# A decoder trunk on one core: the per-layer projection moved to the kernel's start, and the form buffers and filler matmuls dealt out anew

## The chip, the core and the metric

One core of one Trainium2 chip. The time is device microseconds of one execution; several executions are taken, and the median is given. The engines are TensorE (PE, its weight loads PEld), VectorE (DVE), ScalarE (ACT), GpSimd (POOL) and SyncE (SP), each with its own queue of instructions, worked off in order; SP, ACT and POOL also issue transfers between DRAM and on-chip memory.

## What is computed

Two layers over 1024 tokens of width 1024, all in float32:

```python
for i in range(DEPTH):
    h = rms_norm(x, norm_mix_g[i])
    z = h @ w_in[i]
    u_conv, q, k, v, g = jnp.split(z, splits, axis=-1)
    conv_out = conv_module(u_conv, ...)        # gate, 31-tap causal convolution, layer norm, silu
    ret = chunkwise_retention(q, k, v, positions)
    ...                                        # group norm of ret, times silu(g)
    mix = jnp.concatenate([conv_out, ret_out], axis=-1) @ w_out[i]
    x = x + mix
    h = rms_norm(x, norm_ffn_g[i])
    x = x + jnp.square(jax.nn.relu(h @ w_ff1[i])) @ w_ff2[i]
    h = rms_norm(x, norm_ple_g[i])
    x = x + jax.nn.sigmoid(h @ w_ple_gate[i]) * (p[i] @ w_ple_proj[i])
return rms_norm(x, final_norm_g)
```

The last line of a layer is the per-layer input: `p[i]`, 256 wide, goes through the projection `w_ple_proj`, and a gate made from the normed x multiplies it. The projection depends on nothing but inputs.

## The kernel before

The tokens are two halves, A and B, of 512. x stays on chip, feature-major, as `x_0` and `x_1` (8 feature blocks of 128 by 512 tokens each). Every float32 product is made of three matmuls of rounded parts (`mm3`, lines 238 to 240: high by high, high by low, low by high), 128x512 each. A weight tile of 128x1024 is loaded by SP (`stage_weight`, L220, into one of two `stage` buffers), and `split` makes its high part on ACT (`w_hi`, L215) and its low part on DVE (`w_lo`, L216), two buffers each. `gemm` (L242) runs the matmuls of one output block of 512 tokens: 24 for a full depth of 1024, 6 for the projection.

The order of instructions on every engine is fixed when the program is built: a scheduler orders them by priority and dependence, `background(d)` moves a piece d places back or, negative, ahead, and within an engine the order stays as it came out. Tiles come from pools with a number of buffers; a tile that has none free waits until an older one has been read for the last time.

A layer in the order of `run` (L713 on): the norm for mixing; `proj_ab`, v, k, q and g of half A, then of half B, with the convolution on DVE beside them; retention; `w_out` of half A and, later, of half B, with the first 20 (`PRE`) of the 32 `ff1` blocks of half A ahead of the latter. `ff1` writes relu squared to `hid` in DRAM (ACT issues, L537). Then 8 more `ff1` of half A, 4 of half B, the last 4 of half A, and `change(1, 0)` (L776): 4 `ff1` of half B, in whose shade `forms` loads the two halves' `hid` through POOL (L546) and builds seven sums and differences, split in high and low parts (`slots`: q11, t1, t2, q21, t4, t3, q22, L561 to L573). `ff2_chunk` then makes, with seven products in place of eight, one chunk of the second feed-forward matmul, and `pair_weights` prepares the matching sums of its weights (`s_hi`, `s_lo`, L593 to L596). In `ff_forms` (L539) the first four slots are buffers of the pool `h`, which the norms' results use too, and the last three are of the pool `form`.

At the end of a layer comes the per-layer stage: `load_p` (L668), `ple_proj` with 2 weight tiles, both halves, 96 matmuls, its results copied into 16 `pr` tiles (L687), then 8 gate blocks for half A and 8 for half B (`ple`, L693). While the projection runs, the norm of half A (`h3A`, begun in the last feed-forward chunk) is finished on ACT and DVE.

The start has a path of its own. `setup` loads the first half's tokens once more, token-major, into `h` tiles (`x_in`), with the first two weights between them, and then `x_1`; `x_0` follows later (`load_x(0)`). `norm_first` (L312) takes the square sums on ACT, the power on POOL, scales the tokens on DVE, and has PE transpose them (L331) for two quarters of 256 tokens; `proj_ab` of block 0 runs in two parts of 256 columns, so that PE starts on the first quarter while the second is loaded. `gates` holds the instructions behind which the two first weights are split. The other norms (`norm`, L298) square x on ACT (L256), add on DVE (L263), and sum over the partitions on PE; in the form `quick` the row sums go through one short chain of PE (L272), DVE (L275), POOL (L276), ACT and DVE (L277, L278), and a broadcast matmul on PE (L279).

## Time and profile before

| | |
|---|---|
| median of 3 executions | 2421.72 us (2420.17 to 2422.37) |
| the profiled execution | 2422.64 us |
| its span | 2420.9 us |
| mean granted clock of TensorE | 0.997 |
| PE busy | 2380.3 us, 98% |
| DVE busy | 1846.6 us, 76% |
| ACT busy | 1091.3 us, 45% |
| POOL busy | 78.8 us, 3% |

The span runs from the first to the last instruction, and the profiled execution's time is 1.74 us longer. A row of the timeline gives the start, the duration, the engine, the line and the tiles, and in brackets how long the engine had been idle and what ended that. A matmul's duration overlaps the next one's; the distance of two starts is what one costs.

### The profile page before, as it was taken

Reading aid. Unit: us, or ns where it says so; the run is one execution under the profiler, and the core shown is the slowest. Engines: PE = TensorE matmul, PEld = TensorE weight load, DVE = VectorE, ACT = ScalarE, POOL = GpSimd, SP = SyncE. Lnnn points to the kernel's source line nnn. Section 1 sums busy time; section 2 is a strip of 40 time slices with the busy share of each in tenths; the row PEclk is TensorE's granted clock in tenths of the full one; section 3 lists DMA queues with packets and bytes.
Section 4 is the critical chain, followed back from the end, with each engine's and each line's share of the span. In section 5 each row is a group of like instructions: output and inputs, shape, how many; then the busy total and the mean of one; then the engine's idle time right before and its main releaser. Section 6 shows DMA issues by size and latency. Waiting matters only on the chain.

```text
span 2420.9 us, 29197 instructions
## 1 busy us (share of the span) xinstructions
PE 2380.3 (98%) x10916; PEld 1951.7 (81%) x10916; DVE 1846.6 (76%) x3182; ACT 1091.3 (45%) x1766; POOL 78.8 (3%) x120
## 2 busy tenths in 40 slices
PE   8999999999999999999999999999999999999998
PEld 7887888888788787888888888888887888878887
DVE  8999999344567677788999999972626777778888
ACT  5335344534544444445542353463445444444454
POOL 1000000000000000000000000000000000000000
PEclk9999999999999999999999999999999999999999
DMA  5322223434433333332222222244354333333424
GB/s 200 100 70 79 79 77 124 139 109 153 157 122 122 113 122 122 113 120 73 95 96 96 64 89 67 87 132 146 107 165 134 123 120 121 119 115 111 131 78 149
DMA packets 89438, 274.81 MB, mean 114 GB/s; under 512 B 9856, under 2 KB 13952, under 8 KB 89296
## 3 DMA queue, kind: packets, MB, share of 16 engines
q1 hardware_dynamic: 59136, 203.45, 26.7%
q10 hardware_dynamic: 20736, 35.66, 4.4%
q0 software_dynamic: 9424, 33.84, 4.3%
q8 instruction: 85, 1.39, 0.2%
q14 instruction: 57, 0.47, 0.1%
HBM read 235.17 MB, written 37.75 MB: 113 GB/s over the span
## 4 chain that ended last, share of the span: by engine, by line
PE 56%; DVE 17%; issue 15%; DMA 7%; ACT 3%; POOL 1%; POOLq 0%; DVEq 0%; ACTq 0%
PE ps_mm L239 17%; PE ps_mm L238 17%; PE ps_mm L240 17%; DVE conv_acc L367 4%; DVE w_lo L216 4%; DMA stage<-in_wts_dram 3%; DMA h<-hid 3%; DVE h L216 2%; DMA hid<-tmp 1%; ACT w_hi L215 1%; PE ps_ret L238 1%; PE ps_ret L239 1%; PE ps_ret L240 1%; POOL gn_rs L502 1%; DVE ftmp L568 1%
## 5 line engine op out<-in xcount | busy, mean ns | idle before, releaser
L238 PE MATMUL ps_mm<-h,w_hi 128*128 128x512 f32 (+1 forms) x2208 | 854.9, 387 | 0.1
L240 PE MATMUL ps_mm<-h,w_lo 128*128 128x512 f32 (+1 forms) x2208 | 853.4, 387 | 1.4 <-DVE w_lo L216 1.3
L239 PE MATMUL ps_mm<-h,w_hi 128*128 128x512 f32 (+1 forms) x2208 | 853.4, 387 | 0.0
L215 ACT CAST w_hi<-stage 128x1024 fp32r<-128x1024 f32 (+1 forms) x368 | 375.2, 1019 | 647.4 <-PE ps_mm L239 441.9
L216 DVE TENSOR_TENSOR w_lo<-stage,w_hi 128x1024 fp32r<-128x1024 f32 (+1 forms) x368 | 434.3, 1180 | 190.2 <-ACT w_hi L215 189.4
L240 PEld LDWEIGHTS ps_mm<-h,w_lo 128*128 128x128 f32 x2208 | 415.5, 188 | 84.5 <-DVE w_lo L216 3.2
L238 PEld LDWEIGHTS ps_mm<-h,w_hi 128*128 128x128 f32 x2208 | 415.6, 188 | 80.9 <-ACT h L332 0.4
L239 PEld LDWEIGHTS ps_mm<-h,w_hi 128*128 128x128 f32 x2208 | 415.6, 188 | 80.4
L367 DVE SCALAR_TENSOR_TENSOR conv_acc<-u,cw,conv_acc 128x512 f32<-128x512 f32 x480 | 340.6, 747 | 2.5
L238 PE MATMUL ps_mm<-w_hi,h 128*128 128x512 f32 x384 | 150.5, 392 | 0.0
L239 PE MATMUL ps_mm<-w_lo,h 128*128 128x512 f32 x384 | 150.3, 391 | 0.0
L240 PE MATMUL ps_mm<-w_hi,h 128*128 128x512 f32 x384 | 150.2, 391 | 0.0
L256 ACT ACTIVATE ntmp<-x 128x256 f32<-128x256 f32 x208 | 81.6, 414 | 86.4 <-DVE ntmp L263 35.8
L593 DVE TENSOR_TENSOR ftmp<-stage 128x256 f32<-128x256 f32 x56 | 23.8, 425 | 95.8 <-DMA stage<-in_wts_dram 95.7
L215 ACT CAST h<-htmp 128x256 fp32r<-128x256 f32 x176 | 66.8, 407 | 49.2 <-DVE htmp L307 48.6
L215 ACT CAST s_hi<-ftmp 128x1024 fp32r<-128x1024 f32 x56 | 58.9, 1051 | 63.9 <-DVE ftmp L596 47.9
L238 PEld LDWEIGHTS ps_mm<-w_hi,h 128*128 128x128 f32 x384 | 72.1, 188 | 14.5
L239 PEld LDWEIGHTS ps_mm<-w_lo,h 128*128 128x128 f32 x384 | 72.3, 188 | 14.3
L240 PEld LDWEIGHTS ps_mm<-w_hi,h 128*128 128x128 f32 x384 | 72.1, 188 | 14.4
L536 ACT ACTIVATE tmp<-tmp 128x512 f32<-128x512 f32 x128 | 81.1, 634 | 3.4
L216 DVE TENSOR_TENSOR s_lo<-ftmp,s_hi 128x1024 fp32r<-128x1024 f32 x56 | 68.5, 1224 | 18.1 <-ACT s_hi L215 17.9
L263 DVE TENSOR_TENSOR ntmp<-ntmp 128x256 f32<-128x256 f32 x176 | 73.8, 419 | 3.9 <-ACT ntmp L256 1.9
(204 smaller groups left out, 3202.1 us busy)
## 6 DMA issues: line engine op xcount, KB each, us to landing
stage<-in_wts_dram SPq DMA_DIRECT2D x368, 512.0 KB, 3.6
hid<-tmp ACTq DMA_DIRECT2D x128, 256.0 KB, 3.2
h<-hid POOLq DMA_DIRECT2D x36, 512.0 KB, 5.0
raw<-hid POOLq DMA_DIRECT2D x28, 512.0 KB, 4.8
x<-in_xT_dram SPq DMA_DIRECT2D x4, 1024.0 KB, 10.5
h<-in_x_dram SPq DMA_DIRECT2D x4, 512.0 KB, 5.4
tmp<-in_pT_dram SPq DMA_DIRECT2D x8, 256.0 KB, 3.0
out_dram<-x SPq DMA_DIRECT2D x16, 128.0 KB, 1.9
```

Of the source, the lines that this page charges most:

```text
L215: self.nc.scalar.copy(hi, src)
L216: self.nc.vector.tensor_sub(lo, src, hi.bitcast(F32))
L238: mm(ps, lhsT=wh, rhs=xh, start=start, stop=False)
L239: mm(ps, lhsT=wh, rhs=xl, start=False, stop=False)
L240: mm(ps, lhsT=wl, rhs=xh, start=False, stop=stop)
L256: square = lambda k, out: nc.scalar.activation(out, self.x[k][h][:, cs], AF.Square)
L263: nc.vector.tensor_add(sq, acc, sq)
L367: nc.vector.scalar_tensor_tensor(acc, u[:, j:j + HT], w(j), acc, ALU.mult, ALU.add)
L502: nc.gpsimd.tensor_tensor(rs, rs, self.npow[:, 0:HEADS], ALU.pow)
L536: nc.scalar.activation(r, r, AF.Square)
L568: sub(a, r21, b)
L593: nc.vector.tensor_add(blk(s, 0), blk(st, 0), blk(st, 3))
```

## The change

It drops the token-major input, `norm_first`, `gates` and the two-part `proj_ab`. The kernel now begins with p of layer 0 and the whole projection of layer 0, whose results are written to DRAM (`prd`); `x_0` and `x_1` are loaded feature-major and half A's first norm is the common one in the form `quick`. Layer 0's per-layer stage makes half of layer 1's projection (first weight tile) and stores it through a pool `prs` of two buffers, and each per-layer stage reads its stored results back through POOL. Layer 1's stage makes the other half there. Of the slots, q11, t1 and q21 now lie in the pool `form`, and t2, t4, t3, q22 in `h`. 16 `ff1` of half A stand ahead of half B's `w_out` in place of 20, and 8 in place of 4 between half B's first four and `change(1, 0)`.

```diff
-PRE = 20
+PRE, SPARE = 16, 8
...
     def weight(self, L, t):
-        first = bool(self.next_weights)
-        st = self.next_weights.pop(0) if first else self.stage_weight(L, t)
+        st = self.stage_weight(L, t)
...
-    def proj_ab(self, L, h, hs, cb, parts=1):
...
+    def proj_ab(self, L, h, hs, cb):
+        nc = self.nc
+        psb = self.gemm(self.weight(L, T_AB + 2 * cb), hs)
+        psa = self.gemm(self.weight(L, T_AB + 2 * cb + 1), hs)
...
     def ff_forms(self):
-        quads = [self.quad()[0] for _ in range(KEPT)]
-        quads += [self.pools["form"].tile([P, 4, HT], F32R, name="form") for _ in range(FORMS - KEPT)]
+        old = [self.quad()[0] for _ in range(KEPT)]
+        new = [self.pools["form"].tile([P, 4, HT], F32R, name="form") for _ in range(FORMS - KEPT)]
+        quads = [new[0], new[1], old[0], new[2]] + old[1:]
...
+    def ple_proj(self, L, pps, i, pool):
+        w = self.weight(L, T_PROJ + i)
+        pr = []
+        for h in range(NH):
+            for m in range(4):
+                ps = self.gemm(w, pps[h], 2 * m)
+                t = self.tile(pool)
+                self.nc.scalar.copy(t, ps)
+                pr.append(t)
         return pr
+
+    def ple_proj_out(self, L, pps, i, pool):
+        for n, t in enumerate(self.ple_proj(L, pps, i, pool)):
+            self.nc.scalar.dma_start(out=self.prd[L][n // 4][4 * i + n % 4], in_=t)
+
+    def ple_proj_in(self, L, h, m):
+        t = self.tile("pr")
+        self.nc.gpsimd.dma_start(out=t, in_=self.prd[L][h][m])
+        return t
...
-                if L > 0:
+                if L == 0:
+                    pps = [self.load_p(0, 0, "gen")]
+                    self.load_x(0)
+                    pps.append(self.load_p(0, 1, "gen"))
+                    self.load_x(1)
+                    self.load_tables()
+                    for i in range(2):
+                        self.ple_proj_out(0, pps, i, "gen")
+                    h1[0] = self.norm(0, V_MIX, 0, True)
+                else:
                     norm_b()
...
-                for m in range(PRE, NMB - 4):
+                for m in range(PRE, NMB - SPARE):
                     self.ff1(L, m, h2[0], hids[0])
                 self.right_pools(raw=2)
                 for m in range(4):
                     self.ff1(L, m, h2[1], hids[1])
-                for m in range(NMB - 4, NMB):
+                for m in range(NMB - SPARE, NMB):
                     self.ff1(L, m, h2[0], hids[0])
...
-            with self.stage_pools(pp=8, pr=16):
-                pr = self.ple_proj(L, [self.load_p(L, h) for h in range(NH)])
+            with self.stage_pools(pp=8, pr=16, prs=2):
+                pps = [self.load_p(1, h, "pp") for h in range(NH)]
+                if L == 0:
+                    self.ple_proj_out(1, pps, 0, "prs")
+                    pr = [[self.ple_proj_in(0, h, m) for m in range(KB)] for h in range(NH)]
+                else:
+                    pr = [[self.ple_proj_in(1, h, m) for m in range(4)] for h in range(NH)]
+                    more = self.ple_proj(1, pps, 1, "pr")
+                    pr = [pr[h] + more[4 * h:4 * h + 4] for h in range(NH)]
                 h3B = self.norm(1, v0 + V_PLE, SLACK)
```

How the order on the engines moves is shown at three places; the changed kernel's lines have numbers of their own (its L223 to L225 are `mm3`, L257 and L264 the row sums and the broadcast of `quick`, L206 and L207 `split`, L292 `htmp`, L640 the copy of a projection result, L646 its store). A number behind a tile's name tells its instances apart.

PE at the start of the kernel, before: transposes of the first quarter, then `proj_ab` in 256 columns with the second quarter's transposes among its matmuls, then the first of 512 columns (block 1).

```order
L331 MATMUL ps_mm<-ident,h 128x128 x16
L238 MATMUL ps_mm<-h,w_hi 128x256
L239 MATMUL ps_mm<-h,w_hi 128x256
L240 MATMUL ps_mm<-h,w_lo 128x256
...
L331 MATMUL ps_mm<-ident,h 128x128 x6
L238 MATMUL ps_mm<-h,w_hi 128x256 x2
...
L238 MATMUL ps_mm<-h,w_hi 128x512
```

PE at the start, changed (`gen` holds the parts of p, `h` the normed x; `w_hi_204` and `w_hi_290` are the projection's two weights, 512 and 543 those of block 0):

```order
L257 MATMUL ps_aux_378<-ones32_111,ntmp_399 128x1 x2
L264 MATMUL ps_ret_406<-ntmp_405,ones32_111 128x256
L223 MATMUL ps_mm_208<-gen_166,w_hi_204 128x512
L224 MATMUL ps_mm_208<-gen_167,w_hi_204 128x512
L223 MATMUL ps_mm_217<-gen_166,w_hi_204 128x512
L225 MATMUL ps_mm_208<-gen_166,w_lo_205 128x512
...
L224 MATMUL ps_mm_357<-gen_187,w_hi_290 128x512
L225 MATMUL ps_mm_357<-gen_186,w_lo_291 128x512
L257 MATMUL ps_aux_444<-ones32_111,ntmp_465 128x1 x2
L264 MATMUL ps_ret_472<-ntmp_471,ones32_111 128x256
L223 MATMUL ps_mm_516<-h_374,w_hi_512 128x512
L223 MATMUL ps_mm_547<-h_374,w_hi_543 128x512
```

The row sums and the broadcast of the first quarter now stand ahead of the projection, those of the second quarter behind its last matmul, and `proj_ab` of block 0 behind both.

DVE around the change-over to the second feed-forward matmul of layer 0, before. `h_5366` and 5367, 5368 are q11, t1, t2; `form_5370` to 5372 are t4, t3, q22; `w_lo_5378`, 5384, 5433, 5474 belong to the four `ff1` of `change`.

```order
L216 TENSOR_TENSOR w_lo_5378<-stage_5375,w_hi_5377 128x1024
L561 TENSOR_TENSOR ftmp_5393<-raw_5387,h_5366 128x1024
L216 TENSOR_TENSOR w_lo_5384<-stage_5381,w_hi_5383 128x1024
L562 TENSOR_TENSOR ftmp_5394<-raw_5388,ftmp_5393 128x1024
L216 TENSOR_TENSOR h_5366<-h_5366 128x1024
L216 TENSOR_TENSOR h_5367<-ftmp_5393,h_5367 128x1024
L216 TENSOR_TENSOR h_5368<-ftmp_5394,h_5368 128x1024
L216 TENSOR_TENSOR w_lo_5433<-stage_5430,w_hi_5432 128x1024
...
L216 TENSOR_TENSOR form_5370<-ftmp_5438,form_5370 128x1024
L216 TENSOR_TENSOR w_lo_5474<-stage_5471,w_hi_5473 128x1024
...
L216 TENSOR_TENSOR form_5371<-ftmp_5479,form_5371 128x1024
L216 TENSOR_TENSOR form_5372<-raw_5388,form_5372 128x1024
```

Changed: `form_5572` to 5574 are q11, t1, q21, `h_5568` to 5571 are t2, t4, t3, q22; `w_lo_5291` and 5536 belong to the first and the last of the eight `ff1` of half A there, 5580 and 5586 to the first two of `change`.

```order
L207 TENSOR_TENSOR w_lo_5291<-stage_5288,w_hi_5290 128x1024
L515 TENSOR_TENSOR ftmp_5595<-raw_5589,form_5572 128x1024
L207 TENSOR_TENSOR form_5572<-form_5572 128x1024
L207 TENSOR_TENSOR form_5573<-ftmp_5595,form_5573 128x1024
...
L207 TENSOR_TENSOR form_5574<-form_5574 128x1024
...
L207 TENSOR_TENSOR w_lo_5536<-stage_5533,w_hi_5535 128x1024
L207 TENSOR_TENSOR w_lo_5580<-stage_5577,w_hi_5579 128x1024
L207 TENSOR_TENSOR h_5568<-ftmp_5596,h_5568 128x1024
L207 TENSOR_TENSOR h_5569<-ftmp_5640,h_5569 128x1024
...
L207 TENSOR_TENSOR w_lo_5586<-stage_5583,w_hi_5585 128x1024
L207 TENSOR_TENSOR h_5570<-ftmp_5681,h_5570 128x1024
L207 TENSOR_TENSOR h_5571<-raw_5590,h_5571 128x1024
```

The first subtraction moved from behind the first weight of `change` to behind the first of eight weights of half A, and the last form from behind the fourth weight of `change` to behind its second.

ACT in the per-layer stage of layer 0, before (`pr` the copies of projection results, `h` the casts of half A's norm, `w_hi_9294` the first gate's weight):

```order
L687 COPY pr_9022<-ps_mm_9015 128x512
L215 CAST h_8657<-htmp_8779 128x256
L215 CAST h_8658<-htmp_8732 128x256
L687 COPY pr_9031<-ps_mm_9024 128x512
L215 CAST h_8657<-htmp_8783 128x256
...
L687 COPY pr_9049<-ps_mm_9042 128x512
L215 CAST h_8658<-htmp_8799 128x256
L215 CAST h_8658<-htmp_8803 128x256
L215 CAST w_hi_9294<-stage_9292 128x1024
L687 COPY pr_9058<-ps_mm_9051 128x512
L687 COPY pr_9073<-ps_mm_9066 128x512
L215 CAST h_8658<-htmp_8807 128x256
```

Changed (`prs` the two store buffers, `pr_1_...` the stores to DRAM, `h_8859` and `h_8860` the casts of half A's norm, `w_hi_9496` the second gate's weight):

```order
L640 COPY prs_9218<-ps_mm_9211 128x512
L206 CAST h_8860<-htmp_8930 128x256
L646 DMA pr_1_0_2_132<-prs_9218 128x512
L640 COPY prs_9227<-ps_mm_9220 128x512
L206 CAST h_8859<-htmp_8981 128x256
...
L206 CAST w_hi_9496<-stage_9494 128x1024
L640 COPY prs_9254<-ps_mm_9247 128x512
L206 CAST h_8860<-htmp_8997 128x256
L640 COPY prs_9263<-ps_mm_9256 128x512
L646 DMA pr_1_1_2_140<-prs_9254 128x512
L646 DMA pr_1_1_3_141<-prs_9263 128x512
L206 CAST h_8860<-htmp_9001 128x256
```

Half as many copies stand among the casts, each pair of them behind the store of the pair before, and some of the casts now stand behind the last copies.

## Rows read from the trace of the kernel before

**Rows 1.** The page, parts 1 and 2: busy time of each engine, and the busy share of DVE in 40 slices of 60.5 us, in tenths.
```profile
PE 2380.3 (98%) x10916; PEld 1951.7 (81%) x10916; DVE 1846.6 (76%) x3182; ACT 1091.3 (45%) x1766; POOL 78.8 (3%) x120
...
DVE  8999999344567677788999999972626777778888
```

**Rows 2.** The waits of the whole execution: engine, tile and line that waited, what ended the wait; us in total, times, the longest.
```profile
PE ps_ret L238 <- ACT w_hi L215: 8.4, 5, 3.3
...
PE ps_mm L331 <- DVE ln_rs L322: 7.2, 1, 7.2
...
PE ps_ret L476 <- DVE rtmp L472: 4.0, 8, 0.7
```

**Rows 3.** The timeline of PE at the start: start in us, duration, engine, line, operation, tiles, count, and in brackets the idle time before it and what ended it.
```profile
7.20 0.69 PE L331 MATMUL ps_mm<-ident,h 128*128 128x128 f32 x2 [7.20 <-DVE ln_rs L322]
...
11.45 0.56 PE L238 MATMUL ps_mm<-h,w_hi 128*128 128x256 f32 x1
...
14.30 0.28 PE L239 MATMUL ps_mm<-h,w_hi 128*128 128x256 f32 x1
...
26.76 0.40 PE L238 MATMUL ps_mm<-h,w_hi 128*128 128x512 f32 x1
```

**Rows 4.** The timelines of PE, DVE, POOL and ACT around the entry into the second feed-forward matmul, in layer 0 (618 to 650 us) and, for PE, in layer 1 (1839 to 1844 us); columns as before. `ACTq` is the issue of a transfer by ACT.
```profile
618.27 1.05 POOL L546 DMA_DIRECT2D h<-hid  x2 [12.50 <-PE ps_mm L240]
...
625.55 1.23 DVE L561 TENSOR_TENSOR ftmp<-raw,h 128x1024 f32<-128x1024 f32 x1 [7.95 <-DMA h<-hid]
...
626.42 0.39 PE L239 MATMUL ps_mm<-h,w_hi 128*128 128x512 f32 x1
627.97 0.50 PE L240 MATMUL ps_mm<-h,w_lo 128*128 128x512 f32 x1 [1.15 <-DVE w_lo L216]
...
645.11 0.39 PE L239 MATMUL ps_ret<-h,w_hi 128*128 128x512 f32 x1
645.34 0.39 PE L240 MATMUL ps_ret<-h,w_lo 128*128 128x512 f32 x1
649.02 0.77 PE L238 MATMUL ps_ret<-h,w_hi 128*128 128x512 f32 x1 [3.29 <-ACT w_hi L215]
...
644.37 0.33 ACTq L537 DMA_DIRECT2D hid<-tmp  x1
...
1839.54 0.39 PE L240 MATMUL ps_ret<-h,w_lo 128*128 128x512 f32 x1
1843.17 0.50 PE L238 MATMUL ps_ret<-h,w_hi 128*128 128x512 f32 x1 [3.25 <-ACT w_hi L215]
```

**Rows 5.** Stretches of the start: length, then busy us and count of PE, PEld, DVE, ACT and POOL, the granted clock of TensorE (1.00 is full), the busy share of the DMA engines, and GB/s.
```profile
0.00:10.00 10.00, 2.42 (x10) 1.86 (x10) 3.55 (x11) 5.42 (x9) 4.78 (x15) 1.00 0.82 310
10.00:20.00 10.00, 9.84 (x65) 8.96 (x63) 6.38 (x15) 6.42 (x15) 1.99 (x4) 1.00 1.04 385
```

**Rows 6.** Groups of instructions of the whole execution, shapes kept apart: line, engine, operation, tiles and shapes, count | busy us, mean ns of one | idle time before them.
```profile
L216 DVE TENSOR_TENSOR w_lo<-stage,w_hi 128x1024 fp32r<-128x1024 f32 x312 | 381.0, 1221 | 190.2 <-ACT w_hi L215 189.4
...
L256 ACT ACTIVATE ntmp<-x 128x256 f32<-128x256 f32 x208 | 81.6, 414 | 86.4 <-DVE ntmp L263 35.8 <-DVE x L666 16.2 <-DVE x L699 15.2
...
L216 DVE TENSOR_TENSOR h<-htmp,h 128x256 fp32r<-128x256 f32 x176 | 68.4, 420 | 0.8 <-ACT h L215 0.6
L215 ACT CAST h<-htmp 128x256 fp32r<-128x256 f32 x176 | 66.8, 407 | 49.2 <-DVE htmp L307 48.6
L307 DVE SCALAR_TENSOR_TENSOR htmp<-x,vec,rstd 128x256 f32<-128x256 f32 x144 | 64.7, 480 | 0.2
...
L687 ACT COPY pr<-ps_mm 128x512 f32<-128x512 f32 x32 | 18.6, 582 | 6.8 <-PE ps_mm L240 6.4
...
L195 DVE SCALAR_TENSOR_TENSOR ret<-ret 128x512 f32<-128x512 f32 x14 | 9.6, 686 | 0.0
```

**Rows 7.** The chain of a norm that PE, DVE, POOL and ACT pass on to one another, at the end of the execution (timeline, columns as before): its first link, the row sums of PE, and its last, the broadcast.
```profile
2411.63 0.61 PE L272 MATMUL ps_aux<-ones,ntmp 128*128 128x1 f32 x4 [1.34 <-ACT ntmp L256]
...
2413.70 1.19 PE L279 MATMUL ps_ret<-ntmp,ones 128*128 128x256 f32 x2 [1.47 <-ACT ntmp L278]
```

**Rows 8.** Stretches right behind the two long waits of PE, in layer 0 and in layer 1; columns as in the stretches of the start.
```profile
649.00:652.50 3.50, 3.48 (x8) 2.80 (x9) 2.85 (x5) 0.98 (x2) 0.00 (x0) 0.51 0.22 79
652.50:656.00 3.50, 3.50 (x16) 2.82 (x15) 0.58 (x2) 1.16 (x2) 0.53 (x1) 1.00 0.73 234
1843.80:1847.20 3.40, 3.40 (x10) 2.63 (x9) 3.26 (x6) 0.92 (x2) 0.53 (x1) 0.51 0.21 80
```

**Rows 9.** The timeline of ACT around a table load.
```profile
25.38 1.28 ACT L349 ACT_TABLE_LOAD   x1
26.67 0.60 ACT L349 ACTIVATE tmp<-ps_mm 128x512 f32<-128x512 f32 x1
```

**Rows 10.** Transfers: tiles, queue, count, KB each, median us from issue to landing.
```profile
hid<-tmp ACTq DMA_DIRECT2D x128, 256.0 KB, 3.2
h<-hid POOLq DMA_DIRECT2D x36, 512.0 KB, 5.0
```

**Rows 11.** The per-layer stage of layer 0: PE's first projection and first gate matmul, and DVE's last subtraction of half A's norm (timeline).
```profile
1101.18 0.40 PE L238 MATMUL ps_mm<-pp,w_hi 128*128 128x512 f32 x1
...
1114.90 0.43 DVE L216 TENSOR_TENSOR h<-htmp,h 128x256 fp32r<-128x256 f32 x1
...
1123.58 0.40 PE L238 MATMUL ps_mm<-h,w_hi 128*128 128x512 f32 x1
```

More of the change, by code (lines that the diff above doesn't have):

```diff
@@ L714, in run @@
         self.setup()
-        self.gates = []
-        h1 = [(self.quad()[1] + self.quad()[1], self.quad()[1] + self.quad()[1]), None]
-        self.norm_first(V_MIX, 0, h1[0])
-        with self.tc.issue_after(self.first_pow):
-            self.load_tables()
+        self.prd = [[[self.dram.tile([P, HT], F32, name=f"pr_{L}_{h}_{m}") for m in range(KB)]
+                     for h in range(NH)] for L in range(DEPTH)]
+        h1 = [None, None]
         mA = None
@@ L724, in norm_b @@
             def norm_b():
-                with ExitStack() as order:
-                    if L == 0:
-                        order.enter_context(self.tc.issue_after(self.gates[-1][0]))
-                    h1[1] = self.norm(1, v0 + V_MIX, SLACK)
+                h1[1] = self.norm(1, v0 + V_MIX, SLACK)
             def conv_out_a():
```

74 lines of the change are left out of this document (7 added, 67 removed).

## The prediction

> **What bounds the kernel now.** I read the page first: TensorE is busy for 98% of the span [rows 1], so time is gained only where PE waits or runs slowly, and every microsecond of work laid on its path is paid in full. VectorE is full in the first 400 us (the digits 8 and 9) and has room later. Then PE's list of waits [rows 2]: the two large entries are 7.2 us for the first transposes, and 8.4 us in 5 waits for `w_hi`, two of which, of 3.3 us, are the entries into the second feed-forward matmul, one per layer. Then PE's timeline at those places. At the start the transposes begin at 7.20, the first matmul of `proj_ab` at 11.45, the rate has doubled by 14.30, when the rows are 0.28 long and not 0.56, and the first 512-wide matmul of block 1 starts at 26.76 [rows 3]. At the entry of layer 0 PE loses time at 627.97 and at 649.02, behind DVE and ACT work that began when `h` came from DRAM at 625.55, 7.95 us late; POOL had issued that load only at 618.27, when its buffer came free [rows 4]. A full-speed 512-wide matmul starts every 0.227 us (from the two starts 645.11 and 645.34 in [rows 4]). The profiled execution took 2422.64 us, 0.92 above the median of 2421.72; the sum is made on the former and 0.9 taken off at the end. A measurement of this kernel can tell about 0.2%, 4.8 us, from no change.
>
> **The start: +12.5 us.** The mark is the start of block 1's first matmul. Before it is at 26.76, and the 96 projection matmuls that are moved here cost 96 x 0.227 = 21.8 us in their old place, so an equal start would have it at 48.5.
> - Loads. The SP queue brings two p tiles, x_0, two p tiles, x_1, then the weights. x_0 ends at 2.6 MB, a projection weight at 5.8 MB. The old stream moved 3.1 MB by 10 us and then 385 GB/s [rows 5]: x_0 by about 9.5, the constants that POOL loads taking their share, and the weight by 10 + 2.7/0.385 = 17.
> - First quarter's norm. In the new order it stands ahead of the projection on PE and its `h` pieces ahead of the weight's split on ACT and DVE. From 9.5: the last squares and adds, with two p casts between them, some 2.5 us (four squares of 0.41 and the adds behind them) [rows 6]; the chain from the row sum to the broadcast matmul, 2.07 us at the end of this kernel, 2411.63 to 2413.70 [rows 7], and that matmul, 0.6: 14.7, with 0.5 of rotary work in DVE's queue 15.2. Ahead of the first `w_lo` stand eight `htmp` of 0.48 and six subtractions of 0.42 [rows 6], 6.4 us: 21.6, and 1.22 for `w_lo`: 22.8. So the projection does not begin when its weight lands but about 5 us later.
> - Projection. Three matmuls need `w_hi` alone, 93 more take 21.1 us. PE comes out of idleness; after the 3.29 us wait at 649.02 it issued 8 matmuls in 3.5 us at a granted clock of 0.51, against 16 in the next 3.5 us [rows 8], a loss of 3.5 − 8 x 0.227 = 1.7 us. I take 1.5: end at 45.4.
> - Second quarter's norm. All its PE work stands behind the 96th projection matmul, so its chain is bare: 2.07 + 0.6 for the broadcast + 0.48 `htmp` + 0.41 cast + 0.15 of hand-overs = 3.7 us. 49.1.
> - Block 0, now 48 matmuls of 512 columns: 10.9 us, 60.0. For its clock I add 1.0 of the 1.7, since the first matmuls are paced by the arriving pieces anyway: 61.0. The Trainium skill, "TensorE: Matmul & The Clock Gate", section "HAM oscillation — how this bites in real kernels", says that a matmul stretch behind a long wait for data begins throttled; by it the whole 1.7 would be paid and the start would be +13.2, no row showing a wait of just this kind.
> - A table load and a sine stand between two of the second quarter's casts on ACT, 1.28 + 0.6 us, and two squares. The three k-pieces cast by then keep PE busy for 3 x 6 x 0.227 = 4.1 us, against 3.2 until the next: hidden. In the trace the sigmoid at 26.67 follows its table load (25.38, 1.28 us long) at once [rows 9]. The Trainium skill, "ScalarE: Activation LUTs", section "What ACT_TABLE_LOAD costs", gives 2.66 us with a drain; by that estimate the cover would be 0.5 us short and the start +13.0. The row shows no such drain, and I go by the row.
>
> 61.0 − 48.5 = **+12.5**. Bounds: +9 if the weights are split as they land (22.8 becomes 19.2); +14.5 with both clock terms whole and 1 us more of DVE queue. The store of the 16 results is off the path: a tile of `gen` comes back each 8 results, 10.9 us, against 0.58 + 0.33 + 3.2 [rows 6, 10].
>
> **The entries of the second feed-forward matmul: −11.6 us.** The form slots that are loaded first are now tiles of the pool `form`, free since the stage began, not `h` buffers that half A's last ff1 readers hold; and eight ff1 of half A, not four, stand between half B's first four and the change-over. In the new DVE order five of the seven forms stand ahead of the weight of the change-over's second ff1 and the last two right behind it; before, the first subtraction stood there and the last form behind the fourth weight. So I let 627.97, 649.02 and the wait of layer 1 go whole: layer 0 has 627.97 − 626.42 − 0.23 = 1.3, 649.02 − 645.34 − 0.23 = 3.45 and the 1.7 of slow clock, 6.5; layer 1 has 1843.17 − 1839.54 − 0.23 = 3.4 and 3.4 us at a clock of 0.51 [rows 4, 8], 1.7 again, so 5.1. The next in line is the second `w_hi` of the chunk, whose cast stands behind the pair sums of DVE; I see it about 0.5 us early, from the order and the durations. Bounds −13 (small waits at later chunks go too) and −7.
>
> **The per-layer stages: +1.5 us.** Half of the projection that covered the norm of half A there is gone, 10.9 us. Before, that norm's last subtraction started at 1114.90, 13.7 us after the first projection matmul at 1101.18, and the first gate matmul at 1123.58 [rows 11]; the gate now comes at 10.9, and uses its last k-piece at 15.7. In layer 1 that just holds, but for a `w_lo` in between: +0.5. In layer 0 the eight results go through two buffers to DRAM, copy 0.58, issue 0.33, landing 3.2 [rows 6, 10], about 4.0 us a pair, and the copies are mixed with the norm's casts on ACT: the seventh copy starts 1.4 + 3 x 4.0 = 13.4 us after the first projection matmul, the cast behind it ends at 14.4, and the gate's fifth k wants it at 13.6: +0.8, taken as +1.0. Bounds 0 and +6: with a landing of 5.0, as the loads of `h` show [rows 10], a pair takes 5.8 and the cast ends at 19.8. The 24 loads back ride POOL's queue, which is busy for 3% of the span [rows 1]: nothing.
>
> **Mixing of layer 0: −1 us.** Rotary angles (14 operations of 0.69 [rows 6] and a few shorter ones, some 11 us of a full DVE) now lie under the projection. PE's waits for DVE products there are small (4.0 us in 8 for `rtmp` over both layers [rows 2]), so little comes back. Bounds −4 and +2.
>
> Sum: 12.5 − 11.6 + 1.5 − 1 = +1.4; 2422.64 + 1.4 − 0.9 = **2423 us**.
>
> **Rivals.**
> - *The start is paid less and the mixing stage gives more* (faster). Condition: DVE gets through the first quarter's pieces earlier than I count, and its lead of 11 us ends more of the waits behind it. For: DVE is at 8 and 9 there. Against: the order ties `w_lo` to the pieces. Start +10, mixing −4, stages +0.5: −5.1, 2416.5.
> - *The two store buffers* (slower). If a store takes 5 us instead of 3.2, ACT holds the norm's casts and PE's gates wait some 6 us. For: loads of twice the size show 5.0 [rows 10], and 16 loads run at the same time. Against: stores of just this size show 3.2 [rows 10]. It decides from about 3.0 on. +5 on the stage and +1 on the start: +7.4, 2429.
> - *A new wait takes the entry's place* (slower). The forms are early, but `w_hi` of the next tile is late by the pair sums or by its load; from 0.5 us of lateness PE waits. With 1.8 us of wait and 1.7 of clock left at each entry, −11.6 becomes −4.6: 2430.
> - That the projection is not the kernel's first PE work is in the order already, and so in the forecast.
>
> **How the numbers follow.** The forecast has 0.55, the first rival 0.18, the buffers 0.17, the new wait 0.10. The forecast's own bounds, 2418 to 2428, put 0.48 within 0.2% (2417 to 2426.5), 0.01 below and 0.06 above; the first rival gives 0.16 to faster and 0.02 to the middle, the second 0.15 to slower and 0.02 to the middle, the third all to slower. Faster 0.17, same 0.52, slower 0.31. The range reaches to the rivals' values with a little beyond: 2414 to 2431.
>
> **What would show it.** The first projection matmul at 21 to 23 us, the last near 45, a gap on PE of 3 to 4 us right behind it, and block 1 at 60 to 62. At both entries no PE wait over 0.5 us and no slice at a clock of 0.5. In layer 0's per-layer stage a PE gap of about 1 us in the first gate. Wrong it is if block 1 starts before 57 or after 64, if a `w_hi` wait of over 1 us stands at an entry, or if the first gate of layer 0 loses over 3 us.

## The result and the profile after

The change is slower: 2446.25 us (median of 5 executions, 2442.70 to 2449.26) against 2421.72; the ratio is 1.0104, interval 1.0093 to 1.0115. The forecast was 2423 with a range up to 2431. The profiled execution took 2443.44 us, 20.8 more than that of before, and 2.8 less than its own median.

The first lines of the page of the changed kernel, to be read against [rows 1]:

```profile
PE 2385.5 (98%) x10848; PEld 1947.1 (80%) x10848; DVE 1860.5 (76%) x3212; ACT 1097.5 (45%) x1781; POOL 91.2 (4%) x142
...
PE   5999999999999999999999999999999999999998
```

PE is as busy as before, so the page alone shows only the 5 of the first slice. The list of PE's waits (columns as in [rows 2]) shows more:

```profile
PE ps_aux L257 <- DVE ntmp L248: 16.9, 2, 16.1
...
PE ps_mm L223 <- ACT w_hi L206: 4.9, 1, 4.9
PE ps_mm L223 <- ACT h L206: 4.2, 3, 2.9
PE ps_mm L225 <- DVE w_lo L207: 3.9, 4, 1.8
...
PE ps_ret L223 <- ACT w_hi L206: 1.7, 3, 0.9
```

The 8.4 us for `w_hi` at the feed-forward products of [rows 2] are 1.7; new are 16.1 and 4.9 at the start, 2.9 for `h` in a gate, and 1.8 for `w_lo`. Setting the starts of the same matmuls of both traces side by side, with the moved projection's 21.8 and 10.9 us taken off, puts the difference in its places (their sum is within 0.3 us of the 20.8):

| place | forecast | measured |
|---|---|---|
| start, to block 1 | +12.5 | +18.1 |
| mixing of layer 0 | −1 | −0.9 |
| the two entries | −11.6 | −8.8 |
| per-layer stage of layer 0 | +1.0 | +7.9 |
| per-layer stage of layer 1 | +0.5 | about 0 |
| everything else | 0 | +4.8 |

**The start.** PE's timeline, against [rows 3]:

```profile
16.15 1.01 PE L257 MATMUL ps_aux<-ones,ntmp 128*128 128x1 f32 x4 [16.15 <-DVE ntmp L248]
19.23 1.22 PE L264 MATMUL ps_ret<-ntmp,ones 128*128 128x256 f32 x2 [2.06 <-ACT ntmp L263]
25.37 0.80 PE L223 MATMUL ps_mm<-gen,w_hi 128*128 128x512 f32 x1 [4.92 <-ACT w_hi L206]
...
30.40 0.40 PE L225 MATMUL ps_mm<-gen,w_lo 128*128 128x512 f32 x1
...
50.23 0.50 PE L257 MATMUL ps_aux<-ones,ntmp 128*128 128x1 f32 x4
52.19 0.70 PE L264 MATMUL ps_ret<-ntmp,ones 128*128 128x256 f32 x2 [1.46 <-ACT ntmp L263]
53.90 1.01 PE L223 MATMUL ps_mm<-h,w_hi 128*128 128x512 f32 x2 [1.01 <-ACT h L206]
...
66.59 0.39 PE L223 MATMUL ps_mm<-h,w_hi 128*128 128x512 f32 x1
```

What stands ahead of 25.37, on ACT and then on DVE:

```profile
13.22 1.03 ACT L241 ACTIVATE ntmp<-x 128x256 f32<-128x256 f32 x3 [1.26 <-DMA x<-in_xT_dram]
...
24.27 1.04 ACT L206 CAST w_hi<-stage 128x1024 fp32r<-128x1024 f32 x1
```

```profile
25.64 1.22 DVE L207 TENSOR_TENSOR w_lo<-stage,w_hi 128x1024 fp32r<-128x1024 f32 x1
```

x_0 is there at 13.1 and not at 9.5. From there to the end of the first `w_lo`, 26.86, it takes 13.7 us where 13.3 was counted, and the idle stretch behind the projection (50.23 to 53.90) is the 3.7 of the forecast. Both clock terms were taken too small. From 25.37 to 30.40 PE starts 11 matmuls, most of them 0.43 us apart. Counted as in the forecast, from the end of the first `w_lo` at 26.86 to the end of the projection at 50.23, 93 matmuls take 23.4 us, 2.3 more than 93 x 0.227, where 1.5 was taken. Of this, 1.7 are the slow stretch (8 matmuls from 26.90 to 30.40), and 0.5 comes from the other 85, which are 0.233 us apart and not 0.227; why, no run shows. Behind the idle stretch PE starts 8 matmuls in 3.40 us at a granted clock of 0.54 (fourth row of the stretches below), about the lower of its two levels, 1.2 GHz, a loss of 3.40 − 8 x 0.227 = 1.6 where 1.0 was taken. The Trainium skill, "TensorE: Matmul & The Clock Gate", section "HAM oscillation — how this bites in real kernels", says that a stretch of matmuls behind a long wait for data begins throttled; the trace agrees, with 1.6 of the 1.7. My reason for charging less, that arriving pieces pace the first matmuls anyway, is not borne out. Stretches, columns as in [rows 5]:

```profile
0.00:10.00 10.00, 0.00 (x0) 0.00 (x0) 1.76 (x7) 2.49 (x3) 4.12 (x14) 1.00 0.78 270
10.00:20.00 10.00, 1.79 (x6) 1.43 (x6) 6.21 (x16) 4.94 (x14) 1.23 (x1) 1.00 0.99 369
25.00:30.00 5.00, 4.63 (x10) 3.31 (x11) 5.00 (x10) 2.96 (x6) 0.00 (x0) 1.00 0.45 115
...
53.90:57.30 3.40, 3.40 (x8) 2.45 (x9) 2.53 (x7) 3.38 (x8) 0.00 (x0) 0.54 0.00 0
57.30:61.00 3.70, 3.70 (x17) 3.01 (x16) 3.35 (x8) 1.63 (x6) 0.00 (x0) 0.96 0.15 28
1137.00:1148.00 11.00, 11.00 (x48) 8.63 (x47) 7.70 (x19) 4.73 (x10) 7.74 (x15) 1.00 0.85 314
```

The first 10 us brought 2.7 MB, not 3.1, and by 13.1, when x_0 was complete, 2.7 + 3.1 x 0.369 = 3.8 MB had come, not the 2.6 that stand in SP's queue up to its end: transfers issued later had their share of the rate. ACT's table load at 55.40, 1.28 us long, left no PE wait, as forecast.

**The entries.** PE, POOL and DVE at the place of [rows 4], layer 0:

```profile
633.61 0.39 PE L224 MATMUL ps_mm<-h,w_hi 128*128 128x512 f32 x1
635.34 0.50 PE L225 MATMUL ps_mm<-h,w_lo 128*128 128x512 f32 x1 [1.34 <-DVE w_lo L207]
```

```profile
625.06 0.53 POOL L500 DMA_DIRECT2D raw<-hid  x1 [12.18 <-DMA hid<-tmp]
```

```profile
630.41 1.23 DVE L516 TENSOR_TENSOR ftmp<-raw,ftmp 128x1024 f32<-128x1024 f32 x1 [5.62 <-DMA raw<-hid]
631.67 1.23 DVE L522 TENSOR_TENSOR ftmp<-form,ftmp 128x1024 f32<-128x1024 f32 x1
632.93 1.23 DVE L207 TENSOR_TENSOR form<-form 128x1024 fp32r<-128x1024 f32 x1
634.07 2.35 DVE L207 TENSOR_TENSOR w_lo<-stage,w_hi 128x1024 fp32r<-128x1024 f32 x2
```

The waits of before are gone. But a subtraction waits 5.62 us on DVE for the second `raw` load, and the lower part of a weight stands behind it: PE loses 1.5 us here and 1.9 at the same place of layer 1. Later chunks and stages add small amounts.

**The per-layer stage of layer 0.** ACT, then PE:

```profile
1144.80 0.59 ACT L640 COPY prs<-ps_mm 128x512 f32<-128x512 f32 x1 [3.27 <-DMA pr<-prs]
1145.28 0.41 ACT L206 CAST h<-htmp 128x256 fp32r<-128x256 f32 x1
...
1146.88 0.59 ACT L640 COPY prs<-ps_mm 128x512 f32<-128x512 f32 x1 [1.18 <-DMA pr<-prs]
...
1152.04 0.59 ACT L640 COPY prs<-ps_mm 128x512 f32<-128x512 f32 x1 [3.49 <-DMA pr<-prs]
1152.52 0.41 ACT L206 CAST h<-htmp 128x256 fp32r<-128x256 f32 x1
```

```profile
1152.98 0.56 PE L223 MATMUL ps_mm<-h,w_hi 128*128 128x512 f32 x1 [2.90 <-ACT h L206]
```

The view of the tile `prs` says it in two lines (ACT's idle time before it and how often; landing of its stores):

```profile
  DMA pr<-prs: 8.8, 4
...
DMA to landing us min/median/max: 2.0/5.2/6.6
```

The stores take 5.2 us in the median and not 3.2; ACT waits 8.8 us for their buffers, the casts of `h` stand behind it, and PE waits for a cast and then runs at a granted clock of 0.55 from 1152.9 to 1156.9. While it happens the transfers move 314 GB/s (row 1137 to 1148 above). Beside the stores run 16 loads of `pr`, ten of which POOL issues in one go, the other six by 1148.8:

```profile
1137.28 5.29 POOL L650 DMA_DIRECT2D pr<-pr  x10 [49.47 <-DVE h L207]
```

### The profile page after: what moved, and what is told of

It is laid out like the page before. It is cut to its first block, busy times and chain, and to the rows that moved or that the text cites. A ratio compares the mean times of both kernels' runs of the same rounds, so it can differ in the third digit from the quotient of the medians.

```text
span 2441.7 us, 29225 instructions
## 1 busy us (share of the span) xinstructions
PE 2385.5 (98%) x10848; PEld 1947.1 (80%) x10848; DVE 1860.5 (76%) x3212; ACT 1097.5 (45%) x1781; POOL 91.2 (4%) x142
## 3 DMA queue, kind: packets, MB, share of 16 engines
q8 instruction: 85, 1.39, 0.2%
## 4 chain that ended last, share of the span: by engine, by line
PE 61%; DVE 17%; issue 12%; DMA 6%; ACT 2%; POOL 1%; DVEq 0%; SPq 0%; ACTq 0%; POOLq 0%
PE ps_mm L223 18%; PE ps_mm L225 18%; PE ps_mm L224 18%; DVE conv_acc L320 4%; DVE w_lo L207 4%; DMA stage<-in_wts_dram 2%; DMA form<-hid 2%; PE ps_ret L223 1%; PE ps_ret L224 1%; PE ps_ret L225 1%; DVE form L207 1%; POOL gn_rs L455 1%; ACT w_hi L206 1%; DVE h L207 1%; DVE ntmp L248 1%
## 5 line engine op out<-in xcount | busy, mean ns | idle before, releaser
L223 PE MATMUL ps_mm<-h,w_hi 128*128 128x512 f32 (+1 forms) x2096 | 815.4, 389 | 4.3 <-ACT h L206 4.2
L225 PE MATMUL ps_mm<-h,w_lo 128*128 128x512 f32 (+1 forms) x2096 | 814.0, 389 | 3.9 <-DVE w_lo L207 3.9
L224 PE MATMUL ps_mm<-h,w_hi 128*128 128x512 f32 (+1 forms) x2096 | 814.5, 389 | 0.1
L206 ACT CAST w_hi<-stage 128x1024 fp32r<-128x1024 f32 (+1 forms) x368 | 375.0, 1019 | 623.9 <-PE ps_mm L224 403.2
L207 DVE TENSOR_TENSOR w_lo<-stage,w_hi 128x1024 fp32r<-128x1024 f32 (+1 forms) x368 | 433.5, 1178 | 164.7 <-ACT w_hi L206 163.6
L225 PEld LDWEIGHTS ps_mm<-h,w_lo 128*128 128x128 f32 x2096 | 395.1, 188 | 84.1 <-DVE w_lo L207 5.8
L223 PEld LDWEIGHTS ps_mm<-h,w_hi 128*128 128x128 f32 x2096 | 394.5, 188 | 84.4 <-ACT h L206 6.9
L224 PEld LDWEIGHTS ps_mm<-h,w_hi 128*128 128x128 f32 x2096 | 394.9, 188 | 80.4 <-DVE h L207 2.1
L223 PE MATMUL ps_mm<-w_hi,h 128*128 128x512 f32 x384 | 150.4, 392 | 0.0
L225 PE MATMUL ps_mm<-w_hi,h 128*128 128x512 f32 x384 | 150.3, 391 | 0.0
L241 ACT ACTIVATE ntmp<-x 128x256 f32<-128x256 f32 x224 | 87.5, 414 | 95.4 <-DVE ntmp L248 40.3
L206 ACT CAST h<-htmp 128x256 fp32r<-128x256 f32 x192 | 73.0, 407 | 54.0 <-DVE htmp L292 52.5
L223 PE MATMUL ps_ret<-h,s_hi 128*128 128x512 f32 x224 | 89.2, 398 | 0.1
L206 ACT CAST s_hi<-ftmp 128x1024 fp32r<-128x1024 f32 x56 | 58.8, 1051 | 66.8 <-DVE ftmp L550 50.8
L225 PE MATMUL ps_ret<-h,s_lo 128*128 128x512 f32 x224 | 88.6, 396 | 0.0
L224 PE MATMUL ps_ret<-h,s_hi 128*128 128x512 f32 x224 | 88.5, 395 | 0.0
L248 DVE TENSOR_TENSOR ntmp<-ntmp 128x256 f32<-128x256 f32 x190 | 79.5, 419 | 11.2 <-ACT ntmp L241 9.2
L207 DVE TENSOR_TENSOR s_lo<-ftmp,s_hi 128x1024 fp32r<-128x1024 f32 x56 | 68.5, 1224 | 22.6 <-ACT s_hi L206 22.3
L224 PEld LDWEIGHTS ps_mm<-w_lo,h 128*128 128x128 f32 x384 | 72.2, 188 | 14.5
```

Source lines behind the costliest of these rows:

```text
L206: self.nc.scalar.copy(hi, src)
L207: self.nc.vector.tensor_sub(lo, src, hi.bitcast(F32))
L223: mm(ps, lhsT=wh, rhs=xh, start=start, stop=False)
L224: mm(ps, lhsT=wh, rhs=xl, start=False, stop=False)
L225: mm(ps, lhsT=wl, rhs=xh, start=False, stop=stop)
L241: square = lambda k, out: nc.scalar.activation(out, self.x[k][h][:, cs], AF.Square)
```

## The experiments

Unless said otherwise, a kernel here is the changed kernel with one edit, ratios are against the kernel before, and the changed kernel itself stands at 1.0104.

**1. Eight store buffers** (e1_prs8).
```diff
-            with self.stage_pools(pp=8, pr=16, prs=2):
+            with self.stage_pools(pp=8, pr=16, prs=8):
```


> The changed kernel with eight store buffers (prs) instead of two in the per-layer stage of layer 0. In the changed kernel the first three gates of that stage start 7.9 us later than the shortened projection alone would give, against the kernel before. Theory (two buffers): ACT stands still for a store's landing (3.3, 1.2, 3.5 and 0.9 us before the third to sixth copy) and the casts of half A's norm stand behind it, so with eight buffers these waits go, the loss at the gates falls from 7.9 to under 2 us, and the time falls from 2446 to about 2439. Rival (cover): the projection that hid the norm is 10.9 us shorter, and the norm is late by itself: the loss at the gates stays above 5 us and the time above 2443.

Measured: 2445.06 us, 1.0098 (1.0082 to 1.0114). No wait of ACT for `prs` is left, and the first gate's last matmuls come 6.6 us earlier behind the stage's start than in the changed kernel, so the late norm of the rival is not what held them, although the time is the rival's. But the stores now land in 8.0 to 11.3 us, and the wait came back elsewhere, on DVE:

```profile
1159.16 0.12 DVE L306 MEMSET u<- 128x30 f32 x2 [4.52 <-DMA pr<-prs]
```

Tiles `u` of the next stage lie where `prs` was, so DVE, in order, stops until the last store has read its buffer. PE then waits 3.94 us for sums of half B's norm and runs at a granted clock of 0.50 behind that, and before the third gate is done it is as late as in the changed kernel. The buffers were the place of the wait, not its cause.

**2. The loads behind the stores, by the order of writing** (e2_late_in).
```diff
+        self.stored = self.nc.cur_bb.bb.instructions[-1]
...
+                    with self.tc.issue_after(self.stored):
-                    pr = [[self.ple_proj_in(0, h, m) for m in range(KB)] for h in range(NH)]
+                        pr = [[self.ple_proj_in(0, h, m) for m in range(KB)] for h in range(NH)]
```


> The changed kernel with the 16 loads of stored projection results in layer 0's per-layer stage issued only behind the last store there; two store buffers as in the changed kernel. Theory (traffic): the stores land in 5.9 to 6.6 us in place of 2.0 because 16 loads of 256 KB are in the same engines at 314 GB/s; without them stores land in 2 to 3.3 us, ACT waits under 1.5 us in all for a buffer, the loss at the gates falls from 7.9 to about 1 or 2, and the time to about 2440. Rival (the two buffers are too few even for an undisturbed store): landing falls but ACT still waits 3 us or more, loss at the gates 4 or more. Rival (cover): the loss stays above 5 us.

Measured: 2447.12 us, 1.0106 (1.0088 to 1.0124). The trace shows POOL issuing the loads from 1137.08 as before: the edit moved nothing, so it decides nothing.

**3. Four load buffers in layer 0's stage** (e5_pr4), each load written where its tile is first used (`_Late` issues it when it is asked for), so that at most four buffers are filled ahead and the others wait for gates.
```diff
+class _Late:
...
-            with self.stage_pools(pp=8, pr=16, prs=2):
+            with self.stage_pools(pp=8, pr=16 if L else 4, prs=2):
...
-                    pr = [[self.ple_proj_in(0, h, m) for m in range(KB)] for h in range(NH)]
+                    pr = [_Late(partial(self.ple_proj_in, 0, h)) for h in range(NH)]
```


> The changed kernel with four pr tiles in place of 16 in layer 0's per-layer stage, each stored result loaded back when its gate is near; two store buffers as in the changed kernel. In the run with the loads written behind the stores POOL still issued them at the stage's start, so that run tested nothing; here only four can be under way. Theory (traffic): the stores land in 2 to 3.5 us in place of 5.9 to 6.6, ACT waits under 2 us in all for a store buffer, the third gate starts 1 to 2 us later than the shortened projection gives (7.9 in the changed kernel), and the time falls from 2446 to about 2440. Rival (two buffers too few by themselves): stores land fast, but ACT still waits 4 us or more and the gates lose 4 or more. Rival (cover): ACT does not wait and the gates lose 5 or more all the same.

Measured: 2436.24 us, 1.0067 (1.0052 to 1.0082), 10.0 us less than the change by the medians and 9.0 by the ratios. The same two lines of the tile `prs`:

```profile
  DMA pr<-prs: 2.0, 2
...
DMA to landing us min/median/max: 2.0/2.2/3.6
```

In this run the first load is issued at 1158.43, behind the landing of the last store at 1154.40, so no load of `pr` runs beside a store. With two store buffers as before, the stores land in 2.2 us and ACT waits 2.0. So the cause is the 16 loads that share the transfer engines with the stores; shown by taking them away. The gates come 7.7 us earlier, and the profiled execution is 7.9 us shorter; the rest of the difference is in the executions that were not profiled, whose spread fell from 6.6 to 1.0 us.

**4. The projection's weights loaded right behind the first p tiles, and the norm written between the projection's two halves** (e3_w_first_mid).
```diff
...
                     pps = [self.load_p(0, 0, "gen")]
+                    sts = [self.stage_weight(0, T_PROJ + i) for i in range(2)]
                     self.load_x(0)
...
-                    for i in range(2):
-                        self.ple_proj_out(0, pps, i, "gen")
+                    self.ple_proj_out(0, pps, 0, "gen", sts[0])
                     h1[0] = self.norm(0, V_MIX, 0, True)
+                    self.ple_proj_out(0, pps, 1, "gen", sts[1])
```


> The changed kernel with the two projection weights loaded right behind the first p tiles and ahead of x_0, and half A's first norm written between the two halves of the projection. In the changed kernel the first projection matmul starts at 25.4 us, the last ends at 50.2, block 1 starts at 66.6; before, with the projection's 21.8 us added, it would be 48.5. Theory (arrival): the start is set by what the loads bring first; x_0 landed at 13.1 and the weights at 21.6. Then the projection starts at 6 to 8 us, runs through, ends near 30, and block 1 starts at 45 to 50: 18 us less, 2428. Rival (DVE and ACT work): the pieces of the norm and the rotary angles on DVE set the start whatever comes first; block 1 then starts at 58 or later and the time stays above 2437.

Measured: 2441.19 us, 1.0081 (1.0063 to 1.0099); block 1 at 61.57, the numbers of the rival. The first projection matmul is at 7.52, the last at 34.96, but most of that is given back, first in a wait for the second quarter's squares, and behind it at the clock, where 14 matmuls of block 0 take 6.31 us at a granted clock of 0.51 (second view, columns as in [rows 5]), a loss of 3.1:

```profile
34.96 0.40 PE L225 MATMUL ps_mm<-gen,w_lo 128*128 128x512 f32 x1
42.84 0.98 PE L257 MATMUL ps_aux<-ones,ntmp 128*128 128x1 f32 x4 [7.49 <-DVE ntmp L248]
```

```profile
47.52:53.83 6.31, 6.31 (x14) 4.63 (x15) 5.10 (x15) 5.69 (x13) 0.00 (x0) 0.51 0.25 95
```

**5. The same with the rotary work issued behind the norm** (e6_start_late_rope), and with experiment 3's edit.
```diff
                     h1[0] = self.norm(0, V_MIX, 0, True)
+                    normed = self.nc.cur_bb.bb.instructions[-1]
...
-                    with self.background(600):
+                    with self.background(600), self.tc.issue_after(normed):
```


> The changed kernel with the projection weights loaded first and the norm between the two halves of the projection, as in the run before, the rotary angles put behind that norm on DVE, and the four pr tiles. In the run before the projection ended at 35.2, but PE then waited until 47.5 for the second quarter's norm, whose adds and pieces stood behind the rotary angles on DVE and the result copies on ACT; block 1 started at 61.6. Theory (queue work after arrival): without the rotary angles ahead of it the norm ends earlier; block 1 starts at 54 to 58, 8 to 12 us ahead of the changed kernel's 66.6. Rival (PE's own order): the first quarter's broadcast stands behind four results of the second half on PE at about 29 us whatever DVE does, and block 1 starts at 60 or later. Mixing later loses up to 3 us of what the start gains, since the angles then take DVE while the convolution wants it.

Measured: 2429.76 us, 1.0038 (1.0024 to 1.0052); block 1 at 61.12, so the rotary work was not what held it; PE still waits 5.38 us for the second quarter's squares, and from 47.20 to 53.13 it again runs at a granted clock of 0.50. That is the rival's place (60 or later). The gates gain their 7.7 again.

**6. The same with the norm written ahead of both halves** (e9_norm_prio).
```diff
+                    h1[0] = self.norm(0, V_MIX, 0, True)
+                    normed = self.nc.cur_bb.bb.instructions[-1]
                     for i in range(2):
-                        self.ple_proj_out(0, pps, i, "gen")
+                        self.ple_proj_out(0, pps, i, "gen", sts[i])
-                    h1[0] = self.norm(0, V_MIX, 0, True)
```


> The kernel of e6_start_late_rope with one thing more: block 0's norm is written ahead of both halves of the input projection, so that PE's part of it (the sums of squares, their broadcast, the transposes) lies between the projection's matmuls as soon as x_0 is there, and the rotary table work follows it on DVE. Theory A (what was lost at the start is PE's order: in e6 the first quarter's broadcast stood behind four results of the projection's second half and the second quarter's norm behind all of it, so PE was idle 7 to 9 us before block 1 although the projection had ended by 35): the projection's first matmul stays at 7.5, block 0's first at about 35, block 1 at 47 to 51, and the total 2417 to 2421, 9 to 13 below e6's 2429.8. Theory B (DVE's and ACT's pieces, not PE's order, hold the norm, since casts of x and copies of results stand ahead of them): block 1 stays above 55 and the total above 2424.

Measured: 2429.35 us, 1.0031 (1.0019 to 1.0042); block 1 at 55.87. The results of the projection now wait on ACT behind the casts of the norm:

```profile
32.99 0.40 ACT L271 ACTIVATE ntmp<-ident,norm_rs 128x128 f32<-128x128 f32 x1 [3.34 <-POOL norm_rs L269]
...
38.36 1.55 ACT L648 COPY gen<-ps_mm 128x512 f32<-128x512 f32 x3
```

```profile
38.99 0.79 PE L231 MATMUL ps_mm<-gen,w_hi 128*128 128x512 f32 x1 [4.85 <-ACT gen L648]
```

The numbers are those of the second theory (above 55, above 2424), its reason holds in part: the norm was held by PE's order after all, by 5.2 us, but what took the order's place is ACT, which copies results only behind the casts. Of the 5.2 us, 3.6 were lost again by 456 us: the beginning of the first feed-forward matmul came out in another order, PE waits 1.39 us there for a `w_lo` at 407.72, and up to 411.3 it runs at a granted clock of 0.53. In the total the two kernels can't be told apart.

**7. x_0 loaded first** (e10_x_first).
```diff
-                    pps = [self.load_p(0, 0, "gen")]
                     self.load_x(0)
+                    pps = [self.load_p(0, 0, "gen")]
                     pps.append(self.load_p(0, 1, "gen"))
```


> The changed kernel with one edit: x_0's two loads are issued ahead of the first half's loads of the layer input p, which stand ahead of them in the change. Theory A (x_0's late arrival, 13.1 us where 9.5 was forecast, set the first norm and through it the first projection matmul at 25.4): x_0 lands by 10.5, the first projection matmul comes at 22.5 to 23.5, block 1 at 63.5 to 64.5 (after: 66.6), the total 2 to 3 us below after. Theory B (the projection's weights, landed at 21.6 and 22.8, and their split on ACT and DVE, not x_0, set it): first projection matmul within 1 us of 25.4, block 1 within 1 us of 66.6, the total unchanged within 0.2%.

Measured: 2445.73 us, 1.0099 (1.0084 to 1.0115). What ACT waits for at the start:

```profile
9.82 1.03 ACT L241 ACTIVATE ntmp<-x 128x256 f32<-128x256 f32 x3 [2.49 <-DMA x<-in_xT_dram]
...
22.17 1.04 ACT L206 CAST w_hi<-stage 128x1024 fp32r<-128x1024 f32 x1 [0.42 <-DMA stage<-in_wts_dram]
```

x_0 is 3.4 us earlier and the first projection matmul 2.1 (23.27), as the first theory had it, but block 1 only 1.5 (65.13): now the weight, landed at 22.15, is what comes last. In the changed kernel it landed at 21.55, where the forecast had 17. So both arrivals were forecast too early, and the second was hidden behind the first. In the total the edit can't be told from no change.

**8. to 10. The kernel before with the form buffers and the filler blocks of the change** (e4_b_ff), with the buffers alone (e7_b_forms) and with the blocks alone (e8_b_fill). The diff shows both, the blocks first.
```diff
-PRE = 20
+PRE, SPARE = 16, 8
...
-        quads = [self.quad()[0] for _ in range(KEPT)]
...
+        quads = [new[0], new[1], old[0], new[2]] + old[1:]
```


> The kernel before with the form slots and the filler blocks (PRE 16, SPARE 8) of the change and nothing else. Theory: the change gains at the entries into the second feed-forward matmul what the comparison of the two traces shows there, some 5 us in layer 0 and 4 in layer 1, and this is independent of the start: 2421.7 becomes about 2412 to 2414. Rival: the gain shows in the changed kernel only because its other stages run late; alone the two edits bring under 4 us.

> The kernel before with the new dealing of form slots alone (PRE 20 and the last four ff1 of half A as before). With both edits the entries gained 5.2 and about 4 us and lost 1.3 and 1.9 of it to a new wait of PE for w_lo, behind the first subtraction of the forms, which waits for its load. Theory (the slots alone carry the gain, since the loads no longer wait for a buffer of h): the entry's 3.3 us wait is gone or under 1 us; 2421 becomes 2413 to 2417. Rival (four ff1 of half A are too short a time for the forms): a wait of over 1 us stays at 649 us, and the time is within 3 us of before.

> The kernel before with PRE 16 and SPARE 8 alone, the form slots as before. Theory (the slots carry the gain): the first slots are still buffers of h that the last ff1 of half A hold, so POOL's load and the entry's wait stay where they were relative to the change-over, and the time is within 2 us of before. Rival (the fillers carry it): the waits of 3.3 us at the entries go, and the time falls by 4 or more.

Measured: both 2416.99 us, 0.9987 (0.9977 to 0.9997); buffers alone 2416.55, 0.9985 (0.9974 to 0.9996); blocks alone 2420.53, 0.9998 (0.9989 to 1.0008). The buffers are what works, though both together bring 3.1 us by the ratio and 4.1 by the medians, where the theory had 8 to 10. With the blocks alone the waits of 3.3 us at the entries stay. With both, the new wait for `w_lo` is there as in the changed kernel (1.3 and 1.9 us), and with the buffers alone it is 2.2 and 1.9.

**11. Experiment 8 with one DVE instruction per layer moved** (e11_b_ff_lo): the subtraction that waits for the second `raw` load is issued behind the weight part that it kept waiting (the first added line stands in `weight`, behind the split).
```diff
+            self.last_lo = self.nc.cur_bb.bb.instructions[-1]
...
                     self.ff1(L, m, h2[0], hids[0])
+                    if m == NMB - SPARE + 3:
+                        self.after_lo = self.last_lo
...
-        sub(b, r22, a)
+        with self.tc.issue_after(self.after_lo):
+            sub(b, r22, a)
```


> The kernel of e4_b_ff (the kernel before with the form buffers and filler blocks of the change) with one instruction per layer moved on DVE: the subtraction that needs the second load of raw is issued behind the w_lo of the fourth filler ff1 instead of ahead of it. Nothing else stands in another place. Theory A (the new wait of PE for w_lo at the entry comes from DVE's order alone: the subtraction waits 5.4 and 6.0 us for its load, and the weight's lower part, whose inputs are there, stands behind it): the waits of 1.3 us in layer 0 and 1.9 us in layer 1 go, the time falls by about 3 us below e4's 2417, to some 2414, and the forms are still early enough, so no wait takes their place. Theory B (the weight itself is late: its load lands late behind the raw load, or its upper part is): the waits stay at 1 us or more each and the time is that of e4 within 1 us. Theory C (the forms, now 1.3 us later, arrive late at the first products of the second matmul): the w_lo waits go but a wait of the same size stands at the entry, and the time is again that of e4.

Measured: 2413.84 us, 0.9972 (0.9961 to 0.9984), the fastest kernel of this study; the kernel before took 2421.29 beside it. DVE now:

```profile
591.56 1.23 DVE L216 TENSOR_TENSOR w_lo<-stage,w_hi 128x1024 fp32r<-128x1024 f32 x1 [4.21 <-ACT w_hi L215]
593.42 1.23 DVE L565 TENSOR_TENSOR ftmp<-raw,ftmp 128x1024 f32<-128x1024 f32 x1 [0.63 <-DMA raw<-hid]
```

No wait of PE for `w_lo` is left at either entry, and none has taken its place there. So the new wait came from DVE's order, as the first theory said.

## Why the prediction was wrong

The experiments split the change without the profile. From before to experiment 8 the ratio goes to 0.9987 (forms and blocks: −3.1 us), from there to experiment 3's 1.0067 (the moved projection, without the crowd of loads: +19.4), from there to 1.0104 (the crowd: +9.0). The forecast had −11.6, +12.0 and +1.0 for these: it missed by 8.5, 7.4 and 8.0, three errors of the same sign. Each ratio is known to 2.4 to 3.6 us, so a difference of two to some 4.5. The first of the three is not the entries alone: in the trace of experiment 8 they gain as much as in the changed kernel, within 0.1 us, but the second feed-forward matmuls behind them lose 2.3 us in small waits. Of the signs of being wrong that the prediction named, two came, block 1 after 64 and the first gate of layer 0; a `w_hi` wait at an entry did not. Three steps failed, and the clock was mis-sized:

- **"x_0 by about 9.5 ... and the weight by 17"** failed. It was 13.1 and 21.6. The estimate gave the queue's bytes in their order the whole rate; in the trace everything under way shared it, and the rate of the first 10 us, 310 GB/s in [rows 5], was 270. Of the start's error of 5.6 us, 3.6 came through x_0, 0.4 through the pieces behind it, and 1.6 through the rate of PE, the next point. Taking x_0 first gave back only 1.5 (experiment 7), where the weight became the last to come. The structure of the step was right: the chain behind x_0, the order of `w_lo` behind the `htmp` pieces and the bare second norm took what was counted, within 0.4 us.
- **The two clock terms** (1.5 and 1.0) were mis-sized; they measured 2.3, of which 0.5 lie outside the slow stretch, and 1.6. The bound of +14.5, "both clock terms whole", left out the loads.
- **"landing 3.2"** for the stores failed; it was 5.2 in the median, up to 6.6. The second rival had the mechanism, the place and its sign: a store of 5 us, ACT holding the casts, PE waiting some 6 us. I gave it 0.17 because [rows 10] show 3.2 for stores of the same size; but in experiment 3, beside weight loads alone, the stores of this very stage land in 2.2, and beside the 16 loads in 5.2: the price is set by what runs beside them, and it was taken from a quieter place although "16 loads run at the same time" stood in the same sentence. "The 24 loads back ride POOL's queue ... nothing" priced their issue and not their traffic. Without the loads the stage takes 0.25 us less than before and not 1.0 more (experiment 3), so the cover and the two buffers were counted right, if a little dear.
- **"I let 627.97, 649.02 and the wait of layer 1 go whole"** was right for these three: the layers gained 12.2 gross, the 8.8 of the table and the new waits of 1.5 and 1.9. What failed is that nothing takes their place: I looked for the next late item at `w_hi`, by the pair sums, and it was `w_lo`, behind a subtraction that had moved ahead of its data. With that subtraction issued later (experiment 11) the two entries, up to the second chunk, are 11.6 us shorter than before, so the size was right for entries without the new wait. The order quoted ahead of the prediction shows the first subtraction's move; the later one and its load's release by a store of `hid` I did not follow.
- **Mixing −1** was right (−0.9), **the second quarter's idle stretch** of 3.7 and **the table load** hidden were right, **layer 1's stage** +0.5 was nearly nothing.
- **Not foreseen:** +4.8 us in many small waits of later stages. Of these, 1.8 lie in the second feed-forward matmuls behind the entries, a part that swings: it is +2.3 in experiment 8 and −3.8 in the profiled execution of the blocks alone, whose median is that of before. Another 1.1 lie in layer 1 between the gates and the entry; there all eight kernels with the moved projection lose 1.0 to 1.8 us against before, and the four without it (8 to 11) none, so this part comes with the moved projection. Experiment 6 shows how such waits come and go when another order comes out (3.6 us at the first feed-forward matmul). What makes each of those of the change stays open, as does how much of the 2.8 us between the profiled run and the median is the same stage's traffic.

## What to carry to other kernels

Price a transfer by what is under way beside it, not by the same transfer in a quiet place, and ask of every new burst of loads whose buffer it keeps occupied and which in-order engine waits for that buffer. When a wait is removed by starting work earlier, look on the same engine for the first instruction that now stands ahead of its data: what is queued behind it is the next wait. And a long transfer at the start of a kernel shares the rate with everything issued behind it until it has landed.

## What the runs showed of the hardware

- Stores of 256 KB land in 2.2 us (median) beside weight loads alone (experiment 3), in 5.2 beside 16 loads of 256 KB as well, and in 9.1 when eight of them are issued beside those loads without waiting (experiment 1); the core moved 314 and 317 GB/s from 1137 to 1148 in the latter two.
- Behind 4.9 us of idle time at the start PE runs at about half its rate from 25.37 to 30.40, mostly 0.43 us from matmul to matmul, though the profile's granted clock says 1.00 for 25 to 30; behind the later idle stretch it says 0.54. At the start the distance of the rows tells the clock, not the column.
- A removed wait can come back as clock: in experiment 4 PE ends the projection 15.0 us earlier than in the changed kernel, waits 7.49 us, and loses 3.1 us more behind it at a granted clock of 0.51.
